# New matmul costs in the list scheduler of a two-block transformer kernel

## The chip, the cores and the metric

The kernel runs on one NeuronCore of a Trainium2 chip. The metric is the device time of one execution in microseconds; the kernel before was timed three times. Everything else that is said of time here comes from one profiled execution of the same kernel.

## What is computed

Two transformer blocks, one behind the other, on 512 tokens of width 1024, in float32, with a modulation vector that scales and shifts every norm:

```python
def reference(x, c, ...):
    x = first_block(x, c, ...)           # 2 layers: gated FFN, hybrid mixer, gated FFN
    return second_block(x, c_2, ctx_2, ...)  # 2 layers with 256 context tokens beside

# first block, a layer: each sublayer reads a modulated RMS norm
h = rmsnorm(x, g) * (1.0 + scale) + shift        # shift, scale, gate: columns of silu(c) @ w_mod + b_mod
f = (jax.nn.silu(h @ w_g) * (h @ w_u)) @ w_down  # FFN, 2816 hidden features
# mixer: sliding window attention with sinks, a gated linear recurrence, a short convolution

# second block, a layer: mixer (latent attention, then neighbourhood attention), layer norm,
# gated FFN with a convolution of three taps over the positions, layer norm
h_lat = layer_norm(DEEPNORM_ALPHA * h_lat + g1 * y, ln1_g[i], ln1_b[i])
```

The context tokens go through the first layer of the second block too; the second layer only reads them as keys and values.

## The kernel before

Features lie along the 128 partitions and tokens along the free axis, so the stream of 512 tokens is eight tiles of 128 by 512. Weights come from HBM as float32 blocks of 128 by 512 (256 KB). ScalarE rounds each block to a high part (`wh`, CAST) and VectorE subtracts that to a low part (`wl`), and every product is three TensorE matmuls in the rounded type fp32r: high by high, high by low, low by high (`mm3`, `lin`). A moving operand is 512 or 256 columns wide. 256 columns are half the tokens, which is how a norm over one half runs beside the products of the other (`parts`, `ffn_end`), or all tokens of the context. Transposes through the identity (`ident`) move 128 columns of plain float32. Column sums (`colsum`, tile `acc`) multiply 128 by 128 float32 with a column of ones and have one column.

The attention scores of two heads are grouped by `mm2x`: two matmuls over 128 rows, then two over 64 rows each, for the first block's window attention and the second block's neighbourhood attention.

A norm is a chain over all engines: squares on ScalarE, sums on VectorE or GpSimd (`acc`), the column sum on TensorE, about ten short VectorE operations for the reciprocal root (`rsqrt`, tile `c`), a transpose of that column on TensorE that spreads it over the partitions (`bcast`, `ident,c`), and the scaled and shifted halves on VectorE and ScalarE (`tm`, `hh`, `hl`).

The modulation vectors are products of a vector with large matrices, and they don't run on TensorE. Two 256 KB blocks per step (`mr`) are multiplied with the vector on VectorE, with a running sum, and one of each three products on GpSimd with the sum on ScalarE. Where the context needs its own modulation as well, each block is multiplied twice (`mj`, `b_cc`).

**The order of the work is made by the source.** `Recorder.call` takes every operation down in program order and gives it a cost in ns (`Recorder.cost`, line 178). `Recorder.schedule` (line 285) then simulates the five engines with these costs and a table of latencies between them: each engine, when free, takes the earliest operation of the program whose operands are ready and whose tiles have room. The order in which the simulation starts operations is the order in which `emit` issues them, and on the chip each engine runs its own list in that order, waiting where an operand is late. So a cost changes no instruction, only places in five lists.

The cost of TensorE is also a yardstick for the program order itself. `Recorder.call` sums it in `self.pe`. `Core.run` (line 855) reads the sum after each step of the main stream. It writes one step of the modulations into the program for each `EVERY` = 6150 ns of the main stream's TensorE cost, from 20000 ns on, and steps of the context's stream until these have cost 0.22 of the main stream's (0.2987 during the latent attention and after it); there VectorE's cost counts half. The context's stream starts when the modulation it needs has been written down. A step of the modulations that is needed earlier is written down on demand (`mod`).

Of the kernel before, what the change touches and what calls it, by code (L numbers as in the profile page):

```python
# [13 lines left out]
F32R = mybir.dt.float32r  # L14
# [5 lines left out]
P = 128  # L20
# [49 lines left out]


def parts(T):
    """The tokens in halves: a norm over one runs beside the products of the other."""
    return [slice(i, i + C) for i in range(0, T, C)]


# [9 lines left out]


class View:
    """A part of a tile that gets its memory once the order of the program is known."""

    __slots__ = ("t", "box", "ops", "flat", "raw", "size")

# [57 lines left out]


class Recorder:
    """Takes the program down op by op, then issues it in the order of a list schedule: each engine
    runs the earliest op of the program whose operands are there and whose tiles have room."""

    ENGINES = ("tensor", "vector", "scalar", "gpsimd", "sync")
    LAT = {"tensor": {"tensor": 0},
# [20 lines left out]
    def cost(self, eng, method, a, k):  # L178
        out = a[0]
        n = out.width() if isinstance(out, View) else a[1].width()  # L180
        if eng == "tensor":
            if method == "transpose":
                return 0.84 * n + 2
            x = a[2]
            return max(0.4167 * n, 107) + (3 if n > 256 else 4.5) if x.t.dt == F32R else 220
        if eng == "sync":
            rows = (out.box[1] - out.box[0]) if isinstance(out, View) else P
            return max(450, rows * n * 4 / 360)
        ins = [x for x in a[1:] if isinstance(x, View)]
        psum = any(x.t.psum for x in ins + [out])  # L190
        if method == "reduce_max":
            n = a[1].width()
        if eng == "scalar":
            extra = sum(93 for v in (k.get("bias"), k.get("scale"), k.get("accum_out")) if isinstance(v, View))
            return 95 + 0.75 * n + extra + (0 if psum else 0.08 * n)
        if eng == "vector":
            if method == "reciprocal":
                return 65 + 6.3 * n
            at = 65 + 60 * sum(isinstance(x, View) and x.width() == 1 for x in a[2:])
            if method in ("tensor_scalar", "memset") and not psum:  # L200
                return at + 0.53 * n
            return at + 1.05 * n
        if method == "tensor_scalar":
            return 160 + 0.836 * n + 95 * any(isinstance(x, View) for x in a[2:])
        return 150 + 2.1 * n
# [224 lines left out]


class Lag:
    """Puts the parts of a chain that wait for other engines behind the start of the next ones."""

    def __init__(self, n):
        self.n, self.q = n, []
# [17 lines left out]
class Core:  # L454
# [169 lines left out]
                    self.mcol[(kind + sfx, l, ch)] = cols  # L624

    def first_mods(self):
        """The first shift and scale, finished block by block of features."""
        nc = self.nc
        Sh, G = self.mods[:, 0:8], self.mods[:, 8:16]
        for m in range(8):  # L630
            nc.later = FIRST[0] + FIRST[1] * m
            dots = []
            for ch in range(2):
                d = [self.col(1), self.col(1)]
                for h in range(2):
                    raw = self.t(s="mr")
                    nc.sync.dma_start(raw, self.io["wmod"][0, ch * 8 + m][:, h * 512:(h + 1) * 512])
                    if (2 * ch + h) % 4 in FIRST_POOL:
                        nc.gpsimd.tensor_tensor(raw, raw, self.cb["c", h], op=ALU.mult)
                        nc.scalar.activation(raw, raw, AF.Identity, accum_out=d[h])  # L640
                        continue
                    nc.vector.scalar_tensor_tensor(raw, raw, 1.0, self.cb["c", h], op0=ALU.mult, op1=ALU.mult, accum_out=d[h])
                dots.append(d)
            for ch, out in enumerate((Sh, G)):
                nc.vector.scalar_tensor_tensor(out[:, m:m + 1], dots[ch][0], dots[ch][1], self.bmod[:, ch * 8 + m:ch * 8 + m + 1], op0=ALU.add, op1=ALU.add)
            nc.vector.scalar_tensor_tensor(G[:, m:m + 1], G[:, m:m + 1], 1.0, self.gn[:, m:m + 1], op0=ALU.add, op1=ALU.mult)
        nc.later = 0
        self.mcol["w", 0, 0] = Sh
        self.mcol["w", 0, 1] = G
# [85 lines left out]
        return copy[:, :T]  # L735

    def times(self, p, c):
        """Weights of a softmax times their sum's reciprocal."""
        self.nc.gpsimd.tensor_scalar(p, p, c, 1.0, op0=ALU.mult, op1=ALU.mult)

    def rms(self, x, T, width, eps=1e-6):
# [65 lines left out]
        yield from self.ffn_end(x, dn, prev, hid, gate, T, after)  # L807

    def ffn_end(self, x, dn, prev, hid, gate, T, after):
        """The products with the last two groups of hidden features, for half the tokens and then the others."""  # L810
        gate = self.mod(*gate)
        last = len(FF_CHUNKS) - 1
        a, b = {}, {}
        for sl in parts(T):
            for m in range(KD):
                if m not in a:
                    a[m] = self.wblk(dn, 8 * (last - 1) + m, kind="wend")
                if m // 2 not in b:
                    b[m // 2] = self.wblk(dn, 8 * last + m // 2, kind="wend")
                pd = self.ps()[:, :T]  # L820
                self.lin(pd, a[m] + b[m // 2][m % 2 * 2:m % 2 * 2 + 2], prev + hid, parts=(sl,))
                self.accum(x, m, pd, gate, sl)
                if m % 2:
                    yield
            if after is not None:
                yield from after(sl)
# [26 lines left out]
        return o  # L853

    def run(self, main, side):
        """Takes main down; between its steps, a step of the modulations for every `every` ns of tensor
        work and steps of side up to `share` of main's tensor work."""
        rec = self.nc
        mods, own = BEGIN, 0.0
        due = 0.0  # L860
        mark = rec.pe
        for _ in main:
            own += rec.pe - mark
            due += self.share * (rec.pe - mark)
            while mods + self.every <= own:
                mods += self.every
                next(self.modgen, None)
            while side is not None and due > 0:
                mark = rec.pe + HEAVY * rec.ve
                got = next(side, "end")  # L870
                due -= rec.pe + HEAVY * rec.ve - mark
                if got == "end":
                    side = None
                elif got == "wait":
                    due = 0.0
            mark = rec.pe

    def rms_part(self, l, sub):
        """The modulated norm before a sublayer of the first block, for some of the tokens at a time."""
        out = [self.pair(S, "h") for _ in range(KD)]  # L880

        def part(sl):
# [7 lines left out]
        return out, part  # L890

    def final_part(self):
        """The first block's last norm, then the second block's first modulation."""
        nc = self.nc
        out = [self.pair(S, "a") for _ in range(KD)]
        g = self.gn[:, 48:56]
# [189 lines left out]
                yield from after(sl)  # L1086

    def stack(self, hi, lo):
        """For two heads' halves of 64 rows: each head's high and low parts over one another."""
        nc = self.nc  # L1090
        n = hi.width()
        other = self.t(F32R, s="st")[:, :n]
# [3 lines left out]
        return hi, other  # L1096

    def twice(self, hi):
        """For two heads' halves of 64 rows: each head's rows two times over."""
        nc = self.nc  # L1100
        n = hi.width()
        other = self.t(F32R, s="tw")[:, :n]
# [3 lines left out]
        return hi, other  # L1106

    def mm2x(self, outs, qs, ks, lows):
        """Products of two heads: q's both parts with k's high part in one pass, its high part with
        k's low part in the other."""  # L1110
        te = self.nc.tensor
        rows = (slice(0, 64), slice(64, 128))
        self.nc.group()
# [69 lines left out]
        return output  # L1183

    def centre(self, x, T):
        """Shifts each token by about the mean of its features: a layer norm, which follows, is the
        same for any shift, and its variance loses no digits to a large mean."""
        nc = self.nc
        acc = self.total(x, T, dt=F32R)
        bc = self.ps()[:, :T]  # L1190
# [2 lines left out]
            nc.vector.tensor_tensor(x[k], x[k], bc, op=ALU.subtract)  # L1193

    def ln_part(self, xs, T, l, which, kind, mod, perm=False):
        """A layer norm, and the modulation after it, for some of the tokens at a time."""
        nc = self.nc
        n = C // P
        c0 = (l * 2 + which) * 16
# [61 lines left out]
        return View(b[0][0].t, (0, P, 0, 512)), View(b[0][1].t, (0, P, 0, 512)), b[0][2]  # L1261

    def values(self, cn, wv, ts):
        """Values of 8 heads for 128 tokens: for each head its high and low parts side by side, the
        other way round for odd heads, so that the high parts' rows are the head's own."""
        nc = self.nc
        pv = self.ps()
        for k in range(2):
# [267 lines left out]
            nc.sync.dma_start(View(self.rpbt.t, (0, 16 * P, 24 * cq, 24 * cq + 24), raw=out), View(ed.t, ed.box, raw=inp))  # L1536

    def na_values(self, g, a, ac):
        """Values of two pairs of heads, tokens along the partitions: the four blocks of the latent
        tokens, the three that lie half a block further, and the context's two."""  # L1540
        nc = self.nc
        ws = [self.wblk("nqkv", 12 * g + i) for i in range(4)]
        wide = [tuple(View(w[j][part].t, (0, P, j * P, j * P + 256), (("__getitem__", ((slice(0, P), slice(j * P, j * P + 256)),), {}),))
# [282 lines left out]
```

## Time and profile before

| quantity | value |
|---|---|
| time of three runs, median (lowest to highest) | 3641.77 us (3635.7 to 3643.74) |
| span of the profiled execution, first to last instruction | 3637.0 us |
| TensorE matmuls, busy | 3507.4 us, 96% of the span |
| VectorE busy | 2715.5 us, 75% |
| ScalarE busy | 1822.0 us, 50% |
| GpSimd busy | 794.7 us, 22% |
| DMA, mean | 129 GB/s |

The profile gives the span of its execution; no time of that execution as a whole stands beside it, and the median of the three runs is 4.8 us above the span. A busy matmul overlaps its neighbours: a matmul of 512 columns has a duration of 0.39 us in the records, while the next one starts 0.23 us after it. So the distance between starts is what a matmul costs, and idle time is what is left uncovered.

### The profile page before, as it was taken

How to read it: one execution, taken by the hardware profiler on the slowest of the kernel's cores; microseconds unless marked ns; L12 is line 12 of the kernel's file. 1: busy time of each engine (PE TensorE's matmuls, PEld its weight loads, DVE VectorE, ACT ScalarE, POOL GpSimd, SP SyncE). 2: the span in 40 equal slices, each digit the busy share in tenths (PEclk: the TensorE clock that was granted, in tenths of full speed). 3: DMA queues.
4: the chain of work that ended last, by engine and by line, in shares of the span. 5: the costliest groups of instructions: out<-in, count | busy, mean ns of one | idle time of the engine just before them, and what ended most of it. 6: DMA issues, size and time to landing. Idle time of an engine off the chain costs nothing.

```text
span 3637.0 us, 56958 instructions
## 1 busy us (share of the span) xinstructions
PE 3507.4 (96%) x19814; PEld 3057.1 (84%) x19814; DVE 2715.5 (75%) x5566; ACT 1822.0 (50%) x3939; POOL 794.7 (22%) x848
## 2 busy tenths in 40 slices
PE   6999999999999999999999999999999899989998
PEld 5888979878898879889888988888888888878887
DVE  8966799976597776986444589998667767786566
ACT  5434466455455644754333479785344444454332
POOL 3301142421022330230000034342000523240002
PEclk9999999999999999999999999999999999989999
DMA  9954254655356543553335322124333133233320
GB/s 316 312 157 148 82 184 148 218 182 162 103 191 197 187 132 119 193 160 116 105 108 143 107 59 58 48 68 133 110 96 105 53 100 85 76 94 103 98 87 24
DMA packets 272127, 469.86 MB, mean 129 GB/s; under 512 B 39136, under 2 KB 53472, under 8 KB 271840
## 3 DMA queue, kind: packets, MB, share of 16 engines
q1 hardware_dynamic: 271840, 466.23, 41.9%
q8 instruction: 156, 2.56, 0.3%
q14 instruction: 131, 1.07, 0.1%
HBM read 448.81 MB, written 5.50 MB: 125 GB/s over the span
## 4 chain that ended last, share of the span: by engine, by line
PE 79%; DVE 13%; issue 2%; ACT 2%; DMA 2%; POOL 1%; SPq 0%; POOLq 0%; DVEq 0%; ACTq 0%
PE ps L429 79%; DVE wl L429 2%; DVE c L429 2%; DVE mr L429 1%; DVE acc L429 1%; DVE x L429 1%; DVE mj L429 1%; DVE ptl L429 1%; DMA mr<-in_wmod 1%; POOL P L429 0%; DMA wr<-in_gu 0%; DVE pl L429 0%; DVE al L429 0%; POOL pc L429 0%; DVE yl L429 0%
## 5 line engine op out<-in xcount | busy, mean ns | idle before, releaser
L429 DVE TENSOR_TENSOR wl<-wr,wh 128x512 fp32r<-128x512 f32 (+1 forms) x1182 | 834.4, 729 | 163.0 <-ACT wh L429 134.1
L429 ACT CAST wh<-wr 128x512 fp32r<-128x512 f32 (+1 forms) x1182 | 676.6, 614 | 96.0 <-PE ps L429 61.2
L429 PE MATMUL ps<-hh,wh 128*128 128x512 f32 (+1 forms) x1864 | 692.9, 372 | 3.3 <-ACT wh L429 2.7
L429 PE MATMUL ps<-hl,wh 128*128 128x512 f32 (+1 forms) x1864 | 689.7, 370 | 6.3 <-DVE hl L429 6.2
L429 PE MATMUL ps<-hh,wl 128*128 128x512 f32 (+1 forms) x1864 | 688.0, 369 | 0.1
L429 PE MATMUL ps<-fh,wh 128*128 128x512 f32 (+1 forms) x1344 | 463.5, 345 | 0.0
L429 PE MATMUL ps<-fl,wh 128*128 128x512 f32 (+1 forms) x1344 | 462.0, 344 | 0.2 <-DVE fl L429 0.2
L429 PE MATMUL ps<-fh,wl 128*128 128x512 f32 (+1 forms) x1344 | 461.8, 344 | 0.0
L429 PEld LDWEIGHTS ps<-hl,wh 128*128 128x128 f32 x1864 | 355.4, 191 | 65.0 <-DVE hl L429 9.3
L429 PEld LDWEIGHTS ps<-hh,wh 128*128 128x128 f32 x1864 | 355.5, 191 | 60.8 <-ACT wh L429 3.1
L429 PEld LDWEIGHTS ps<-hh,wl 128*128 128x128 f32 x1864 | 355.1, 190 | 59.7 <-DVE wl L429 1.3
L429 DVE SCALAR_TENSOR_TENSOR x<-ps,mods,x 128x512 f32<-128x512 f32 (+1 forms) x400 | 254.9, 641 | 187.8 <-PE ps L429 186.1
L429 PE MATMUL ps<-ah,wh 128*128 128x512 f32 (+1 forms) x1000 | 366.9, 367 | 0.0
L429 PE MATMUL ps<-al,wh 128*128 128x512 f32 (+1 forms) x1000 | 365.3, 365 | 0.1
L429 PE MATMUL ps<-ah,wl 128*128 128x512 f32 (+1 forms) x1000 | 364.9, 365 | 0.0
L429 POOL TENSOR_TENSOR mr<-mr,b_c 128x512 f32<-128x512 f32 x123 | 179.0, 1457 | 515.1 <-DMA mr<-in_wmod 247.6
L429 DVE SCALAR_TENSOR_TENSOR cv<-ps,ffc,cv 128x511 f32<-128x511 f32 (+1 forms) x264 | 173.3, 659 | 143.7 <-ACT cv L429 140.1
L429 PEld LDWEIGHTS ps<-fl,wh 128*128 128x128 f32 x1344 | 254.7, 190 | 30.0 <-DVE fl L429 0.4
L429 PEld LDWEIGHTS ps<-fh,wl 128*128 128x128 f32 x1344 | 254.6, 189 | 30.1
L429 PEld LDWEIGHTS ps<-fh,wh 128*128 128x128 f32 x1344 | 254.7, 189 | 29.5
L429 ACT ACTIVATE cv<-ps,ffc 128x512 f32<-128x512 f32 (+1 forms) x132 | 93.4, 708 | 314.7 <-PE ps L429 314.0
L429 ACT CAST fh<-s 128x512 fp32r<-128x512 f32 x132 | 81.8, 621 | 299.1 <-DVE s L429 297.0
(332 smaller groups left out, 7115.6 us busy)
## 6 DMA issues: line engine op xcount, KB each, us to landing
wr<-in_gu SPq DMA_DIRECT2D x352, 256.0 KB, 2.9
mr<-in_wmod SPq DMA_DIRECT2D x288, 256.0 KB, 4.2
wr<-in_fin SPq DMA_DIRECT2D x264, 256.0 KB, 2.7
mr<-in_wada SPq DMA_DIRECT2D x192, 256.0 KB, 3.6
wr<-in_dn SPq DMA_DIRECT2D x176, 256.0 KB, 3.1
wr<-in_fout SPq DMA_DIRECT2D x132, 256.0 KB, 2.7
wr<-in_win SPq DMA_DIRECT2D x64, 256.0 KB, 3.3
wr<-in_nqkv SPq DMA_DIRECT2D x48, 256.0 KB, 2.9
```

Of the source, the lines that this page charges most:

```text
L429: getattr(eng, method)(*a, **k)
```

## The change

The diff replaces the cost of a TensorE matmul in `Recorder.cost`. The rest of the diff takes docstrings out and leaves the code as it is.

```diff
             if method == "transpose":
                 return 0.84 * n + 2
             x = a[2]
-            return max(0.4167 * n, 107) + (3 if n > 256 else 4.5) if x.t.dt == F32R else 220
+            if x.t.dt != F32R:
+                return 112
+            rows = a[1].box[1] - a[1].box[0]
+            return max(0.4167 * n, 107) + 13.4 if rows == P else 255
```

In ns, with `n` columns:

| form | cost before | cost after |
|---|---|---|
| fp32r, 512 columns, 128 rows | 216.4 | 226.7 |
| fp32r, 256 columns, 128 rows | 111.5 | 120.4 |
| fp32r, 64 rows, up to 256 columns | 111.5 | 255 |
| float32 column sum, one column | 220 | 112 |
| transpose of 128 columns | 109.5 | 109.5 |

`EVERY`, the shares and every other cost and latency stay as they are. No instruction is added or taken away.

## Rows read from the trace of the kernel before

**Rows 1.** The page's first line.
```profile
span 3637.0 us, 56958 instructions
```

**Rows 2.** Busy time in stretches: us, then PE, PEld, DVE, ACT, POOL, PEclk, DMA.
```profile
400.00:735.00 335.00, 309.67 (x1825) 271.76 (x1823) 323.72 (x749) 191.97 (x467) 122.80 (x97) 0.97 0.54 169
735.00:1200.00 465.00, 463.86 (x2487) 402.41 (x2488) 331.81 (x701) 245.29 (x527) 91.81 (x96) 1.00 0.54 168
1200.00:1320.00 120.00, 110.83 (x544) 93.27 (x543) 105.54 (x212) 69.87 (x152) 58.04 (x49) 0.96 0.48 150
1455.00:1620.00 165.00, 160.52 (x976) 139.63 (x976) 154.49 (x356) 118.54 (x278) 54.14 (x54) 1.00 0.59 186
2100.00:2500.00 400.00, 385.57 (x2643) 352.07 (x2643) 370.34 (x869) 313.25 (x751) 157.09 (x210) 0.99 0.22 64
2845.00:3260.00 415.00, 391.32 (x2553) 346.28 (x2551) 310.09 (x633) 191.88 (x435) 151.82 (x187) 0.96 0.30 83
```

**Rows 3.** Waits of TensorE, whole span: us in total, times, longest.
```profile
PE ps L429 <- DVE c L429: 35.8, 16, 9.9
PE ps L429 <- DVE acc L429: 28.5, 10, 11.1
PE ps L429 <- POOL P L429: 9.3, 10, 2.5
PE ps L429 <- DVE ptl L429: 8.1, 13, 1.9
```

**Rows 4.** Waits of TensorE, first 100 us and last 37 us.
```profile
PE ps L429 <- DVE acc L429: 11.1, 1, 11.1
...
PE ps L429 <- DVE c L429: 7.0, 2, 5.3
```

**Rows 5.** Timeline of TensorE, one norm: start, us, instruction, idle before it.
```profile
2664.18 0.48 PE L429 MATMUL ps<-ah,wh 128*128 128x512 f32 x1
...
2671.34 0.39 PE L429 MATMUL ps<-al,wh 128*128 128x512 f32 x1
2671.56 0.39 PE L429 MATMUL ps<-ah,wl 128*128 128x512 f32 x1
2673.32 0.43 PE L429 MATMUL ps<-ident,c 128*128 128x128 f32 x2 [1.36 <-DVE c L429]
```

**Rows 6.** Timeline of TensorE: 256 columns, then a score group of two heads.
```profile
2939.84 0.28 PE L429 MATMUL ps<-wh,ah 128*128 128x256 f32 x1
2939.96 0.28 PE L429 MATMUL ps<-wl,ah 128*128 128x256 f32 x1
...
2943.24 0.39 PE L429 MATMUL ps<-kh,qh 128*128 128x256 f32 x1
...
2943.98 0.39 PE L429 MATMUL ps<-kc,qh 128*128 128x256 f32 x1
```

**Rows 7.** Timeline of TensorE, four other norms: the matmul that came late.
```profile
415.67 0.69 PE L429 MATMUL ps<-ident,c 128*128 128x128 f32 x2 [4.00 <-DVE c L429]
...
735.20 0.69 PE L429 MATMUL ps<-ident,c 128*128 128x128 f32 x2 [9.92 <-DVE c L429]
...
1295.02 1.01 PE L429 MATMUL ps<-ones,acc 128*128 128x1 f32 x4 [4.43 <-DVE acc L429]
...
1306.63 0.43 PE L429 MATMUL ps<-ident,c 128*128 128x128 f32 x2 [2.28 <-DVE c L429]
```

**Rows 8.** DVE time of modulations by stretch, tile mr, then tile mj.
```profile
400.00:735.00 335.00, 99.92 (x246) 0.97 0.54 169
1200.00:1320.00 120.00, 32.24 (x76) 0.96 0.48 150
1455.00:1620.00 165.00, 23.85 (x68) 1.00 0.59 186
...
400.00:735.00 335.00, 43.54 (x110) 0.97 0.54 169
1200.00:1320.00 120.00, 16.48 (x38) 0.96 0.48 150
```

## The prediction

> **What bounds the kernel now.** I read the table of stretches first, because one share for the whole span hides everything here. Over the 3637.0 us [rows 1] TensorE is the bound nearly throughout: between 735 and 1200 us it is busy for 463.9 of 465 us with VectorE at 71% [rows 2]. There no order of the work can gain or lose anything. The time that an order can touch lies in a few stretches where TensorE falls idle: 400 to 735 us (25.3 us idle, VectorE 97% busy), 1200 to 1320 us (9.2 us idle, VectorE 88%), 1455 to 1620 us (4.5 us, VectorE 94%), the latent attention from 2100 to 2500 us (14.4 us, VectorE 93%) and the neighbourhood attention from 2845 to 3260 us (23.7 us, VectorE 75%) [rows 2]. Next the list of TensorE's waits. It names one kind of cause: TensorE reaches a norm's column sum or its transpose, or a softmax's transpose, before VectorE or GpSimd has delivered. The norm's waits are 35.8 us over 16 for `c` and 28.5 us over 10 for `acc`; those of the softmax that are shown are 9.3 us over 10 for `P` and 8.1 us over 13 for `ptl` [rows 3]. Since each engine runs a fixed list, TensorE stands at such an instruction even when products that could run lie behind it. Of the norm waits, 11.1 us at the start and 7.0 us at the end [rows 4] have no products to fill them, and no cost moves those.
>
> **What the change does to the plan.** No instruction is added or removed; the direct cost is nothing. Five lists are put in another order, because the simulated TensorE gets slower. By how much, and is that true? In the timeline, matmuls of 512 columns start 0.22 to 0.23 us apart [rows 5], and those of 256 columns 0.12 us apart [rows 6]. A score group of two heads (two matmuls over 128 rows, two over 64) takes 0.74 us from 2943.24 to 2943.98 [rows 6]. The costs before make these 0.216, 0.1115 and 0.446 us; the new ones 0.227, 0.120 and 0.751. So the new costs are right for this trace, and the old ones too low by 5%, 7% and 40%. The Trainium skill speaks against the change here: "TensorE: Matmul & The Clock Gate", section "Wait — 56ns, not 53.3ns?", gives warm matmuls of 512 columns a distance of 215.7 ns, which is the old cost; by it the new cost would be 5% too dear, and the case for a gain (the second rival) would have no ground; of the sum below only the small last term would fall away. The rows here show 0.22 to 0.23 us [rows 5], and the measurement decides.
>
> A truer cost of one engine does not by itself make a better order, and this is my main step. **Step one, the cover of the norms.** The plan puts as many products between a norm's column sum and its transpose as fit into the chain's planned length. At 2664 us that cover runs from the matmul at 2664.18 to the one at 2671.56, some 33 matmuls, and the transpose still comes 1.36 us late [rows 5]. In the plan those 33 cost 33 x 0.2164 = 7.14 us; on the chip they take 33 x 0.227 = 7.5 us. The old cost thus carried a hidden reserve of 0.35 us per chain, and even with it the transpose was late. With the new cost the plan fits only 7.14 / 0.2267 = 31.5 matmuls into the same chain; the reserve is gone and TensorE waits 0.35 us longer. I found the same kind of late matmul, with 4.00, 9.92, 4.43 and 2.28 us, at four other places [rows 7]. The middle of the kernel has 35.8 and 28.5 us less 11.1 and 7.0, over some 23 waits [rows 3, 4]. At 0.35 us each that is **+8 us**. Bounds: 0, if the plan itself had nothing left to put in front, and +12 where the cover is of 256 columns and shrinks by 8% (0.5 us each).
>
> **Step two, the softmax chains** lose their reserve in the same way: 23 waits for `P` and `ptl` [rows 3] and as many small ones of other tiles by my estimate from the rest of the list, each with a shorter cover, say 0.2 us: 9 us. But most lie where VectorE is the fuller engine [rows 2], and there a longer wait of TensorE is partly paid back, since VectorE doesn't stop. I take **+4**, bounds 0 to +9.
>
> **Step three, the modulations come earlier.** Their steps are written into the program every 6150 ns of planned TensorE work, and this work grows by 4.8% (512 columns) to 8% (256), some 5.5% for the mix. So at any place of the main stream 5.5% more steps have been written, and the context's stream, which waits for one of them, begins some 20 to 25 us earlier too. (Within the context's stream the share stays: its TensorE cost rises as the main stream's does.) From 400 to 735 us VectorE spends 99.9 + 43.5 = 143.4 us on modulations [rows 8]; 5.5% are 7.9 us. VectorE's idle time there is 335 - 323.7 = 11.3 us [rows 2], much of it in waits too short to use, and the 9.92 us at 735 us [rows 7] says that VectorE is behind its plan at the end of this stretch. I take **+6**, bounds 0 to +10. The same shift helps later. The steps done from 1200 to 1320 us (32.2 + 16.5 = 48.7 us of VectorE, most of them doubled) [rows 8] move about 60 to 70 us forward, into a stretch with 29% of VectorE free [rows 2], and away from the norm whose two matmuls are 4.43 and 2.28 us late [rows 7]: **-5**, bounds -9 to 0, the 9.2 us that TensorE is idle there. From 1455 to 1620 us, 23.9 us of modulations [rows 8] fall by about half: **-2**, bounds -4.5 to 0 by the idle time of TensorE [rows 2]. The queue of SyncE, which issues the loads in the planned order, moves with this: the modulations' loads stand some 5% earlier among the weights; DMA is at 0.48 to 0.59 in these stretches [rows 2], so that costs nothing.
>
> **Step four, fewer wrong turns of the other engines.** In a true plan VectorE and ScalarE reach a product's result less often before it is there. In the stretches that VectorE fills this would count, but VectorE's idle time there is only 11.3 us (400 to 735 us) and 29.7 us (2100 to 2500 us) [rows 2], and one or two of them is what 5% can give back: **-1**, bounds -10 to 0. The score groups, with 40% the form most corrected, lie in the stretch with the most idle time of TensorE, 23.7 us [rows 2], but VectorE has slack there, and I count nothing for them.
>
> **The sum** against the profiled execution: 8 + 4 + 6 - 5 - 2 - 1 = +10 us, so a span of 3647 us; with the 4.8 us that the median lies above that span, **3652 us**. All lower bounds together are -23.5 us and all upper ones +31.
>
> **The rivals.** *Nothing that counts*: the shifts cancel, since most of the span has a TensorE without gaps; 3642 us, within 7. For it: the parts of the sum have both signs. Against it: step one hits nearly every norm on the same side. *Faster*: the plan's TensorE is now true, so a late matmul becomes rarer, and the modulations leave the norm at 1290 to 1306 us and the second mixer. It would take the lower bounds of the later steps (-9 - 4.5) and half of step four's (-5), against +5 left of steps one and two: -13.5, or 3628 us. For it: the late matmuls at 735 and 1295 us stand where modulations crowd VectorE, and a shift of 5% can unlock one of them. Against it: what is late on TensorE is late because VectorE and GpSimd are slower than planned, and slowing the planned TensorE widens that gap. It decides by whether covers shrink at the norms. *Much slower*: the stretch from 400 to 735 us has no reserve on VectorE, and the added 7.9 us of modulations and the earlier context stream delay its norms one after the other, so that the 9.92 us wait doubles: +10 there above step three's 6, or 3662 us. It decides from the point where VectorE is over 99% busy there. *That the change does nothing* is excluded: the costs enter the order and the yardstick.
>
> **How the numbers follow.** Forecast (3652) 0.34, much slower (3662 and above) 0.11, nothing 0.28, faster 0.27. A measurement tells about 0.2% (7 us) from no change. Slower by over 0.2%: 0.45; within: 0.28; faster: 0.27. The range leaves out the ends where all bounds add up, and takes in the faster rival's time and a little of the much slower one's far side: 3625 to 3674 us.
>
> **What would show it.** In the profile after, TensorE's waits for `c` and `acc` in the middle should sum to more than the 46 us of before, with about as many waits; fewer matmuls should lie between the column sums and their transposes; of the 23.9 us of modulations from 1455 to 1620 us [rows 8] about half should be gone; VectorE from 400 to 735 us should be at least as full; and the wait of 4.43 us near 1295 us should shrink. The prediction is wrong if the covers keep their number of matmuls, or if the norms' waits fall in total while the modulations move as said.

## The result: slower by 1.4%

The changed kernel takes 3688.31 us (3684.8 to 3689.96), the kernel before 3640.47 us in the runs beside it: a ratio of 1.0138, with an interval of 1.0126 to 1.0150. The forecast had the direction, but its 3652 us is far off, and 3688 us lies beyond its range. The profiled execution took 3684.8 us, its span 3682.7 us, 45.7 us above that of before [rows 1].

First the page of the kernel after (its span and TensorE's line, busy time and share), and then the mean granted clock of TensorE, before and after.

```profile
span 3682.7 us, 56929 instructions
PE 3523.0 (96%) x19814; PEld 3070.1 (83%) x19814; DVE 2714.8 (74%) x5566; ACT 1810.4 (49%) x3934; POOL 782.8 (21%) x848
```
```profile
core 0: 3637.0 us, clock 0.988
```
```profile
core 0: 3682.7 us, clock 0.984
```

The work is the same: 19814 matmuls, 5566 VectorE instructions. TensorE was busy for 3507.4 us before and is for 3523.0 us now, 15.6 us more for the same matmuls; it was idle for 129.6 us and is for 159.7 us, 30.1 us more. These two make the 45.7 us. The clock accounts for most of the first. The granted clock has two levels here, full and half, so a mean of 0.988 is half speed for 2 x 0.012 x 3637 = 87 us, and a mean of 0.984 for 2 x 0.016 x 3682.7 = 118 us. Work loses half of the time that it spends at half speed, and TensorE stood idle in some of that time. By the clock's stretches in the two traces it worked at half speed for 61 us before and for 87 us after, so 13 of the 15.6 us are the clock's.

The stretches of [rows 2] in the kernel after (us, PE, PEld, DVE, ACT, POOL, clock, DMA). The later ones no longer hold quite the same work.

```profile
400.00:735.00 335.00, 300.25 (x1775) 264.57 (x1775) 324.94 (x756) 189.95 (x474) 122.02 (x100) 0.95 0.53 168
735.00:1200.00 465.00, 456.43 (x2451) 394.99 (x2450) 328.81 (x692) 243.11 (x526) 101.52 (x103) 1.00 0.53 165
1200.00:1320.00 120.00, 109.00 (x522) 90.96 (x522) 106.23 (x215) 61.59 (x136) 45.98 (x42) 0.94 0.55 170
1455.00:1620.00 165.00, 157.73 (x1041) 142.11 (x1041) 141.26 (x323) 101.23 (x231) 39.81 (x39) 1.00 0.47 147
2100.00:2500.00 400.00, 381.02 (x2596) 346.62 (x2595) 352.75 (x845) 309.45 (x746) 139.96 (x201) 0.99 0.21 61
2845.00:3260.00 415.00, 395.69 (x2515) 349.28 (x2513) 298.80 (x596) 192.91 (x426) 135.77 (x168) 0.97 0.30 83
```

TensorE's waits after (us in total, times, longest), to hold against [rows 3], and then two rows of before that [rows 3] doesn't have:

```profile
PE ps L432 <- DVE acc L432: 38.0, 8, 12.3
PE ps L432 <- DVE c L432: 24.4, 15, 5.3
PE ps L432 <- DVE ptl L432: 14.4, 19, 2.6
PE ps L432 <- DVE pl L432: 10.6, 8, 4.4
...
PE ps L432 <- POOL P L432: 6.3, 5, 2.3
...
PE ps L432 <- ACT pth L432: 5.2, 4, 2.8
```
```profile
PE ps L429 <- DVE pl L429: 2.4, 3, 1.1
...
PE ps L429 <- ACT pth L429: 0.8, 2, 0.5
```

The norms' waits for VectorE, `acc` and `c`, sum to 62.4 us after and 64.3 us before: in total they have not grown. The total hides a trade: the 9.92 us at 735 us [rows 7] are gone (no wait for `c` is longer than 5.3 us now), and a wait of 12.28 us for `acc` is new. The waits inside the attentions grew: `ptl` from 8.1 to 14.4 us, `pl` from 2.4 to 10.6 us and `pth` from 0.8 to 5.2 us. Two of the largest new waits sit in the first block's first mixer and at the norm behind it. This is the timeline of TensorE there, after (start, us, instruction, idle before it):

```profile
511.19 0.28 PE L432 MATMUL ps<-ph,vh 128*128 128x256 f32 x1
515.87 0.54 PE L432 MATMUL ps<-pl,vh 128*128 128x256 f32 x1 [4.40 <-DVE pl L432]
...
516.43 0.41 PE L432 MATMUL ps<-ph,vh 128*128 128x256 f32 x1
516.64 0.41 PE L432 MATMUL ps<-pl,vh 128*128 128x256 f32 x1
...
624.79 1.01 PE L432 MATMUL ps<-ones,acc 128*128 128x1 f32 x4 [12.28 <-DVE acc L432]
```

Behind the wait of 4.40 us the matmuls of 256 columns start 0.21 us apart, where 0.12 us is normal [rows 6]: that is the half clock (0.53 is the mean granted clock from 515.87 to 517.00 us). Now ScalarE's last rounding of `ph` ahead of the wait's end, and what VectorE did while TensorE stood for `pl`:

```profile
510.00 0.59 ACT L432 CAST ph<-ps 128x512 fp32r<-128x512 f32 x1 [0.16 <-PE ps L432]
```
```profile
511.77 0.68 DVE L432 TENSOR_TENSOR wl<-wr,wh 128x512 fp32r<-128x512 f32 x1
...
513.58 0.68 DVE L432 SCALAR_TENSOR_TENSOR mj<-mr,b_c 128x512 f32<-128x512 f32 x1
...
514.19 0.69 DVE L432 SCALAR_TENSOR_TENSOR mj<-mr,b_c 128x512 f32<-128x512 f32 x1
...
514.80 0.69 DVE L432 TENSOR_TENSOR ql<-ps,qh 128x512 fp32r<-128x512 f32 x1
515.40 1.01 DVE L432 TENSOR_TENSOR pl<-ps,ph 128x256 fp32r<-128x256 f32 x2
```

The `ph` that `pl` is made from was there at 510.6 us, and VectorE never stood still in the wait. It worked on a weight block that is needed later, on the recurrence (one of the rows left out) and on modulations of the second block (`mj`), and only then on the `pl` that TensorE stood for. The wait of 12.28 us at the norm shows the same. These are VectorE's time and instructions on modulations in that wait (us, VectorE, clock, DMA), and then, before the change, in the same length of time ahead of the same column sum, for which TensorE waited 1.0 us there:

```profile
612.51:624.79 12.28, 6.16 (x12) 0.60 0.28 85
```
```profile
567.09:579.37 12.28, 0.10 (x2) 1.00 0.33 97
```

Half of that wait is modulations between the sums of the norm; the other half is the sums themselves and the updates of `x` that feed them.

### The profile page after: what moved, and what is told of

It reads as the page before. It is cut to its first block, busy times and chain, and to the rows that moved or that the text cites. A ratio compares the mean times of both kernels' runs of the same rounds, so it can differ in the third digit from the quotient of the medians.

```text
span 3682.7 us, 56929 instructions
## 1 busy us (share of the span) xinstructions
PE 3523.0 (96%) x19814; PEld 3070.1 (83%) x19814; DVE 2714.8 (74%) x5566; ACT 1810.4 (49%) x3934; POOL 782.8 (21%) x848
## 4 chain that ended last, share of the span: by engine, by line
PE 53%; DVE 8%; ACT 3%; issue 1%; DMA 0%; POOL 0%; SPq 0%; POOLq 0%; DVEq 0%; ACTq 0%
PE ps L432 53%; DVE c L432 2%; DVE wl L432 1%; DVE x L432 1%; DVE ptl L432 1%; DVE acc L432 1%; DVE pl L432 0%; ACT pth L432 0%; ACT pl L432 0%; DVE al L432 0%; DVE mr L432 0%; DVE cv L432 0%; ACT L432 0%; ACT Qh L432 0%; ACT pc L432 0%
## 5 line engine op out<-in xcount | busy, mean ns | idle before, releaser
L432 DVE TENSOR_TENSOR wl<-wr,wh 128x512 fp32r<-128x512 f32 (+1 forms) x1182 | 844.4, 733 | 172.5 <-ACT wh L432 143.5
L432 PEld LDWEIGHTS ps<-fh,wl 128*128 128x128 f32 x1344 | 255.0, 190 | 30.3
```

Source lines behind the costliest of these rows:

```text
L432: getattr(eng, method)(*a, **k)
```

## The experiments

Every kernel here computes the whole thing; only the simulated costs, and with them the five lists, differ. "Plan" are the costs of the simulated engines, "pace" is the yardstick `self.pe` of `run`. All ratios are to the kernel before beside them, with a 95% interval.

| run | plan | pace | median us | ratio (interval) |
|---|---|---|---|---|
| after | new | new | 3688.3 | 1.0138 (1.0126 to 1.0150) |
| e1 | new | old | 3681.9 | 1.0124 (1.0109 to 1.0139) |
| e2 | old | new | 3644.9 | 1.0026 (1.0015 to 1.0037) |
| e3 | new, all other costs x 1.055 | old | 3663.5 | 1.0075 (1.0060 to 1.0090) |
| e4 | matmuls x 1.015 | old | 3669.3 | 1.0091 (1.0074 to 1.0108) |
| f1 | matmuls x 0.985 | old | 3651.9 | 1.0041 (1.0028 to 1.0054) |
| f2, f3 | jitter of 1.5%, two draws | old | 3639.9, 3637.6 | 1.0012 (1.0003 to 1.0021), 1.0000 (0.9991 to 1.0010) |
| f4 | small forms new | old | 3660.2 | 1.0064 (1.0047 to 1.0081) |
| g1 | wide forms new | old | 3667.5 | 1.0088 (1.0073 to 1.0103) |
| g2 | wide forms new, all others x 1.055 | old | 3657.3 | 1.0060 (1.0045 to 1.0075) |
| g3 | 64 rows new | old | 3646.7 | 1.0026 (1.0015 to 1.0038) |
| g4 | column sums new | old | 3653.8 | 1.0055 (1.0038 to 1.0071) |
| h1, h2 | jitter of 10%, two draws | old | 3657.8, 3656.5 | 1.0056 (1.0041 to 1.0071), 1.0048 (1.0033 to 1.0063) |
| h3 | matmuls x 1.003 | old | 3639.9 | 1.0012 (1.0002 to 1.0021) |
| h4 | new, 0.4 us of reserve | old | 3675.0 | 1.0104 (1.0089 to 1.0119) |
| i1 | matmuls x 0.945 | old | 3636.8 | 1.0001 (0.9992 to 1.0010) |
| i2 | new, with h1's jitter | old | 3696.2 | 1.0162 (1.0145 to 1.0179) |

**Plan or pace?** The edit of e1 keeps the old cost in the yardstick and takes the new one for the simulated operation (`self.new` picks the formula in `cost`); e2 swaps the two values. e3 is e1 with the costs of all other engines, the latencies and the waiting times of the simulation times 1.055, and e4 multiplies the old matmul costs by 1.015 in the plan alone.

```diff
+        self.new = False
         cost = self.cost(eng, method, a, k)
         if eng == "tensor":
             self.pe += cost
+            self.new = True
+            cost = self.cost(eng, method, a, k)
```

> The simulated engines use the new matmul costs; the yardstick that paces modulations and context stream keeps the old ones, so the program order is that of the kernel before. Before 3640 us, after 3688 us. Covers (the slower planned TensorE puts fewer products in front of late norms and softmaxes): 3675 to 3690 us, nearly all of the loss. Pace (modulations and context come 5.5% earlier into stretches that VectorE fills): 3640 to 3655 us. Scatter (the order before was a lucky one and any other order costs some tens of us): 3660 to 3700 us.

> The reverse: the simulated engines keep the old matmul costs, the yardstick counts with the new ones, so modulations and context stream come earlier in the program by some 5.5%. Covers: 3640 to 3650 us. Pace: 3675 to 3690 us. Scatter: 3660 to 3700 us, as for any other order.

> New matmul costs in the simulated engines, old yardstick, and every other cost and latency of the simulation times 1.055, so that TensorE stands to the other engines about as before. Covers (the ratio is what counts): back to 3635 to 3655 us while the run with the new matmul costs alone stays slow. Pace: 3640 to 3655 us like that run. Scatter: 3660 to 3700 us, no nearer to the kernel before than the others.

> Old costs and old yardstick, but the simulated matmuls cost 1.5% more, about a quarter of the change. Covers: a quarter of the loss at most, 3640 to 3655 us. Pace: 3640 us, nothing of it changed. Scatter: 3655 to 3700 us, as much as the whole change.

The plan alone loses 1.24%, the pace alone 0.26%, and both together 1.38%. But e4, with about a quarter of the change, already costs 0.91%, and e3, which restores most of the proportion between the engines, still 0.75%. That is not a loss in proportion to the price; it spoke for a third theory, that any other order costs some tens of us.

**Which way, and how much of it is jitter?** f1 makes the simulated matmuls cheaper (`cost *= 0.985`). f2 and f3 draw a factor for each operation by its place in the program, here with a span of 1.5%. f4 gives only the small forms their new costs.

```diff
         if eng == "tensor":
             self.pe += cost
+            cost *= 1 + 0.015 * (2 * (len(self.ops) * 7919 * 1 % 101 / 100) - 1)
```

> Old costs and yardstick, the simulated matmuls 1.5% cheaper, so that the covers gain reserve. The run with 1.5% dearer ones was 0.9% slower than before. Covers: no slower than before, 3625 to 3645 us. Scatter: as slow as the 1.5% dearer plan, 3655 to 3690 us.

> Old costs and yardstick, each simulated matmul's cost off by a number between -1.5% and +1.5% that is drawn by its place in the program, so that the mean stays. Covers: 3635 to 3650 us, since no chain loses its reserve. Scatter: 3655 to 3690 us, as for the plan that is dearer on all.

> The same with other draws. Covers: 3635 to 3650 us. Scatter: again 3655 to 3690 us, but some 10 us off the first draw.

> Only the small forms get their new costs in the simulated engines (255 ns over 64 rows, 112 ns for the column sums); the wide matmuls and the yardstick keep the old ones. The small forms lie in the two mixers of the first block, at the norms and in the neighbourhood attention. Covers: 3635 to 3655 us, since the products that cover the chains keep their cost. Scatter: 3650 to 3690 us, and also in the latent attention, where no small form stands.

Small jitter costs next to nothing (0.12 and 0.00%), which spoke against the third theory, and matmuls 1.5% cheaper cost 0.41%, which spoke against the first, the covers. The small forms alone, which aren't the products that cover a chain, cost 0.64%.

**Form by form.** g1 and g2 take the wide forms alone, without and with the other costs scaled; g3 and g4 take the two small forms one at a time.

> Only the matmuls of 512 and 256 columns get their new costs in the simulated engines (+4.8% and +8%); the small forms and the yardstick stay. With all forms it was 1.24% slower than before, with the small forms alone 0.64%. Ratio (what counts is how TensorE stands to the other engines in the plan): 0.5 to 0.9% slower, 3654 to 3669 us. Small forms alone to blame: within 0.2% of before. Any shift of the mean costs the same whatever its size (1.5% dearer cost 0.9%, 1.5% cheaper 0.4%): 0.4 to 0.9% too, so this run does not tell that from ratio; the next one does.

> The same, and every other cost and latency of the simulation times 1.055, small forms included, so that the plan is nearly the old one on a slower clock (512 columns 0.7% under it, 256 columns 2.4% over it, transposes unscaled). Ratio: within 0.3% of before, 3630 to 3647 us, while the run with dearer wide matmuls alone is slower by over 0.4%. Any shift costs: 0.4 to 0.9% slower, 3650 to 3669 us.

> Only the matmuls over 64 rows get the new cost (255 for 111.5 ns) in the simulated engines. They stand in the first block's two mixers and in the neighbourhood attention. If the 0.64% of the small forms is theirs: 3652 to 3664 us, lost at the first block's mixers. If it is the column sums': 3632 to 3645 us.

> Only the column sums get the new cost (112 for 220 ns) in the simulated engines, which makes each norm's chain 0.4 to 0.9 us shorter in the plan. If the 0.64% of the small forms is theirs, through fewer products in front of each late transpose: 3650 to 3664 us, spread over the norms. If it is the score groups': 3632 to 3645 us.

Each form alone costs something (0.88, 0.26 and 0.55%), and they don't add up to the 1.24% of all. g2 speaks against the ratio as the whole cause: in proportion its plan is nearly the old one, and 0.60% are lost all the same.

**Any order, or a dearer TensorE?** h1 and h2 are f2 and f3 with a span of 10%; h3 multiplies by 1.003; h4 is e1 with 0.4 us more in the latencies from VectorE, ScalarE and GpSimd to TensorE:

```diff
-           "vector": {"vector": 135, "scalar": 140, "gpsimd": 165, "tensor": 215},
-           "scalar": {"vector": 140, "scalar": 143, "gpsimd": 170, "tensor": 200},
-           "gpsimd": {"vector": 80, "scalar": 80, "gpsimd": 102, "tensor": 170},
+           "vector": {"vector": 135, "scalar": 140, "gpsimd": 165, "tensor": 615},
+           "scalar": {"vector": 140, "scalar": 143, "gpsimd": 170, "tensor": 600},
+           "gpsimd": {"vector": 80, "scalar": 80, "gpsimd": 102, "tensor": 570},
```

> Old costs and yardstick, each simulated matmul off by a drawn number between -10% and +10%, the mean unchanged. Shift of the mean (covers, ratio): within 0.3% of before, 3628 to 3648 us, as the jitter of 1.5%. Any other order: 0.4 to 1.0% slower, 3650 to 3675 us.

> The same with other draws. Shift of the mean: within 0.3% of before. Any other order: 0.4 to 1.0% slower, 3650 to 3675 us, and not the same as the first draw.

> Old costs and yardstick, the simulated matmuls 0.3% dearer. Shift of the mean in proportion (1.5% lost 0.91%): 0.18%, 3643 us. Any other order: it goes by how much of TensorE's list moves, so from nothing to 0.6%, 3636 to 3658 us, out of proportion to the shift.

> New costs in the simulated engines, old yardstick (1.24% slower than before without more), and every result of VectorE, ScalarE and GpSimd reaches the simulated TensorE 0.4 us later, so that the plan puts some 0.4 us more of products in front of each of TensorE's waits, about what the covers were to have lost at a norm. Covers: at least a third of the loss comes back, 3665 us or less, and TensorE's waits for VectorE fall. Any other order: 3655 to 3690 us, with no preference.

With the mean untouched, both draws of 10% lose about 0.5%. So an order that differs enough can cost that much by itself. h3 lies at 0.12%, which fits both forecasts. The reserve in front of TensorE's operands brings back 0.2 of 1.24%, where the cover theory wanted at least a third, and the two intervals overlap: covers are not the main thing.

The last two runs part the two effects. i1 makes the matmuls 5.5% cheaper (`cost *= 0.945`), as far from the old price as the new one is. i2 puts h1's draw on the new costs.

> Old costs and yardstick, the simulated matmuls 5.5% cheaper, so that covers hold 5.5% more products. Covers on top of any other order: less than the 0.5% of the jitter, 3635 to 3654 us. Any other order alone: 0.4 to 1.3% slower, 3650 to 3683 us, since the order moves as far as with the new costs.

> New costs in the simulated engines with the jitter of 10% of the first draw, old yardstick. Covers on top of any other order: 1.0 to 1.5% slower, 3672 to 3690 us, as without jitter, with the loss in the first mixer again. Any other order alone: 0.3 to 0.9%, 3647 to 3669 us, as the jitter of the old costs.

i1 loses nothing. i2 loses 1.62%, more than either forecast, where h1, the same draw on the old costs, loses 0.56%. So on top of the 0.5% of another order, dearer matmuls in the plan cost 0.7% (e1) to 1.1% (i2), and the cheaper ones of i1 seem to give the 0.5% back; that is one run, and f1, cheaper by 1.5%, did lose 0.41%. It fits that e3 and g2, where the ratio of the engines is nearly the old one, come down to 0.75 and 0.60%, near the 0.5% of jitter. e4 with its 0.91% doesn't fit well: by its price it should have lost little more than jitter.

**Where each effect sits.** For this table I took from each trace the distance from every matmul's start to the next one's, less the normal distance of its form (0.227 us for 512 columns, 0.120 for 256, 0.120 also over 64 rows, 0.112 for a column sum, 0.109 for a transpose). The rest, in us, is waiting, half clock and what score groups take beyond that. It is summed between the same amounts of normal matmul work, so that the same stage is compared in each run.

| stage (normal work, us) | before | after | e2 | e1 | i2 | h1 | h2 | i1 |
|---|---|---|---|---|---|---|---|---|
| start (0 to 300) | 28.8 | 29.7 | 27.6 | 28.5 | 29.0 | 28.1 | 28.3 | 28.1 |
| first mixer, its norms (300 to 700) | 40.0 | 54.4 | 44.3 | 53.4 | 58.4 | 45.3 | 42.0 | 43.6 |
| two FFNs, their norms (700 to 1300) | 17.3 | 29.4 | 17.9 | 19.7 | 22.4 | 16.3 | 17.1 | 11.3 |
| second mixer (1300 to 1600) | 12.9 | 14.9 | 8.5 | 25.9 | 19.3 | 15.3 | 21.0 | 8.2 |
| latent attention (2000 to 2500) | 28.5 | 43.0 | 38.9 | 40.1 | 44.5 | 40.6 | 43.1 | 41.1 |
| neighbourhood attention (2700 to 3200) | 62.2 | 64.9 | 60.0 | 67.0 | 67.4 | 58.5 | 57.4 | 55.2 |
| whole span | 201.6 | 246.5 | 207.6 | 248.1 | 253.1 | 216.0 | 220.5 | 198.3 |

Two patterns stand out. In the latent attention all seven other orders of the table lose 10 to 16 us against the one before, dearer, cheaper or jittered: that is the larger part of what another order costs. (The jitter of 1.5%, which is small beside the prices, has 28.2 and 31.8 there; of the other runs h3 and g3 have 28, and f1, f4, g2, g4 and e3 have 34 to 36.) In the first mixer, the second and the neighbourhood attention the runs with a dearer TensorE (e1, i2) lose 13 to 18, 6 to 13 and 5 us, while the cheaper one (i1) loses 4 and gains 5 and 7. The second mixer is the least clear of the three, since one jittered run (h2) loses 8 us there too. The changed kernel itself loses 14.4, 2.0 and 2.7 us in these three. It also loses 12.1 us in the two FFNs, where e1 and e2, with one half of the change each, lose 2.4 and 0.6: from 735 to 1260 us its waits for `ptl` and `pth` sum to 9.5 us, where before has 2.5 us and e1 2.5 us. So that part needs both halves of the change; what makes it was not tested.

How much of each loss is waiting and how much is TensorE's own busy time? Here are TensorE's lines of the pages of e1, e4 and h1:

```profile
PE 3530.8 (96%) x19814; PEld 3075.1 (83%) x19814; DVE 2715.9 (74%) x5566; ACT 1819.3 (49%) x3939; POOL 788.1 (21%) x848
```
```profile
PE 3532.4 (96%) x19814; PEld 3078.1 (84%) x19814; DVE 2719.2 (74%) x5566; ACT 1820.7 (50%) x3938; POOL 789.8 (21%) x848
```
```profile
PE 3509.3 (96%) x19814; PEld 3058.5 (84%) x19814; DVE 2729.2 (75%) x5566; ACT 1822.1 (50%) x3939; POOL 786.0 (22%) x848
```

Their spans are 3683.3, 3673.7 and 3651.3 us. Against before, e1 has 23.4 us more of busy time for the same matmuls and 22.9 us more of idle time, e4 25.0 and 11.7 us, h1 1.9 and 12.4 us. So h1 loses by waiting, while half of e1's loss and two thirds of e4's are busy time, at mean clocks of 0.984 and 0.981 for the 0.988 of before.

**What a dearer TensorE does in the first mixer.** Here is that mixer in seven runs, from the column sum of the norm ahead of it to the first one behind it, 918 to 928 matmuls in each: before, i1, h1, e4, e3, e1 and i2. Each fence has all engines first (us, PE, PEld, DVE, ACT, POOL, clock, DMA), then VectorE's time and instructions on the modulations: the row of the tile `mr`, which holds those that write `mj` too, since they read `mr`. A product is two instructions.

```profile
406.40:579.40 173.00, 160.07 (x922) 137.92 (x920) 162.48 (x384) 109.86 (x278) 66.46 (x61) 0.97 0.43 134
406.40:579.40 173.00, 35.71 (x92) 0.97 0.43 134
```
```profile
406.80:570.60 163.80, 157.31 (x918) 134.85 (x916) 153.99 (x361) 104.54 (x263) 61.09 (x59) 0.99 0.41 129
406.80:570.60 163.80, 33.92 (x88) 0.99 0.41 129
```
```profile
405.90:579.40 173.50, 159.55 (x924) 135.95 (x922) 163.26 (x382) 108.67 (x278) 68.21 (x61) 0.99 0.43 133
405.90:579.40 173.50, 40.64 (x92) 0.99 0.43 133
```
```profile
405.90:589.30 183.40, 165.67 (x928) 141.64 (x926) 167.01 (x393) 110.01 (x279) 67.73 (x62) 0.94 0.42 132
405.90:589.30 183.40, 39.56 (x98) 0.94 0.42 132
```
```profile
406.20:587.90 181.70, 164.28 (x924) 139.28 (x923) 166.64 (x399) 110.03 (x280) 72.64 (x63) 0.96 0.44 138
406.20:587.90 181.70, 40.43 (x104) 0.96 0.44 138
```
```profile
408.90:592.50 183.60, 162.29 (x926) 138.07 (x926) 178.78 (x415) 111.15 (x286) 78.17 (x67) 0.97 0.45 142
408.90:592.50 183.60, 50.40 (x122) 0.97 0.45 142
```
```profile
409.90:601.20 191.30, 169.32 (x923) 143.68 (x923) 180.53 (x413) 112.53 (x288) 78.34 (x67) 0.93 0.43 134
409.90:601.20 191.30, 50.45 (x120) 0.93 0.43 134
```

Before has 92 / 2 = 46 modulation products in this mixer, i1 44, h1 46, e4 49, e3 52, e1 61 and i2 60; the mixer takes 173.0, 163.8, 173.5, 183.4, 181.7, 183.6 and 191.3 us. The program order is the same in all seven. In e1 the plan's VectorE has more room beside the dearer matmuls, and the list puts 15 more products into it that nobody in this mixer needs. On the chip VectorE has little room: it was already busy for 162.5 of 173 us and is now for 178.8 of 183.6. The plan prices a product at 65 + 1.05 x 512 = 603 ns. Most follow one another at 0.61 us (513.58 to 514.19 above), but some take over 1 us each (5 of 45 before, 9 of 60 in e1), so that the mean busy time of one was 35.71 / 46 = 0.78 us before and 50.40 / 61 = 0.83 us in e1.

The count follows the price of the matmuls against that of the other engines. The jittered run with the old mean has the old count, and where the other costs rise too it falls back: e3 has 52 for e1's 61, and g2 has 47 for g1's 55. The time does not follow the count in step. e4 with 3 more products than before loses as much here (10.4 us) as e1 with 15 more (10.6 us), although its VectorE is busy for only 167.0 of 183.4 us; 5.6 of e4's 10.4 us are TensorE's busy time at a clock of 0.94. f4, with the old price on all wide matmuls, has 49 products and takes 183.1 us. e3 gives 9 of the 15 products back and only 1.9 us of the time. At the norm behind the mixer the filling does stand on the path with the plan alone: e1's wait for `acc` is 7.11 us there, and this is VectorE's time on modulations in it.

```profile
585.36:592.47 7.11, 3.80 (x6) 0.71 0.32 106
```

So the filling is shown, and about half of that wait is its work; that it is the main cost of dearer matmuls is not shown. No run held the products in their places while the matmuls got dearer.

The second mixer, in the same cut, before and in e1, has no such filling:

```profile
1460.10:1639.70 179.60, 176.38 (x1088) 154.73 (x1089) 161.08 (x374) 122.29 (x286) 51.58 (x52) 1.00 0.54 169
```
```profile
1475.90:1668.60 192.70, 185.50 (x1092) 162.68 (x1092) 161.41 (x372) 122.11 (x286) 49.67 (x52) 0.95 0.49 155
```

VectorE's work is the same (161 us), and of the 13.1 us 9.1 are busy time of TensorE for nearly as many matmuls: a clock of 0.95 for 1.00, beside idle time that is 4.0 us longer (7.2 for 3.2 us).

## Why the prediction failed

**The direction** was right, and in part for the reason given: VectorE's results come late on TensorE, and a slower planned TensorE made that worse. The size was not: +10 us were forecast, and the span grew by 45.7 us. Two things failed: step one, which was the largest term and came to nothing in the norms' waits, and the sum, which left out the half clock and what another order costs by itself.

**Step one (covers of the norms, +8).** The covers did shrink as said. At the norm of [rows 5], e1 has 30 matmuls in place of 33:

```profile
2704.75 0.48 PE L438 MATMUL ps<-ah,wh 128*128 128x512 f32 x1
...
2711.23 0.39 PE L438 MATMUL ps<-al,wh 128*128 128x512 f32 x1
2711.45 0.39 PE L438 MATMUL ps<-ah,wl 128*128 128x512 f32 x1
2713.08 0.32 PE L438 MATMUL ps<-ident,c 128*128 128x128 f32 x1 [1.24 <-DVE c L438]
```

From 2704.75 to 2711.45 is 6.70 us, 29 distances of 0.23. Yet the transpose is 1.24 us late and not the 1.7 us that the step gives, and over the kernel the norms' waits went from 64.3 to 62.4 us (65.6 us in e1), where I had +8. The step's error was to charge every shorter cover to the path. The chain's own length isn't fixed: it depends on what the plan puts between its VectorE operations. In the wait of 12.28 us these were 6.16 us of modulations, and at 735 us the wait of 9.92 us went away. h4 agrees from the other side: putting the reserve back returned 0.2 of 1.24%.

**Step two (softmax chains, +4)** was mis-sized. `ptl`, `pl`, `pth` and `P` together went from 20.6 to 36.5 us, which is 15.9 us where I had +4 and at most +9. In e1, where the plan alone is new, they have 30.3 us. I priced a cover that is 0.2 us shorter; in the one wait that is opened above, at 515.87 us, VectorE's list had other work in front of the result.

**Step three (pace, +6 - 5 - 2).** e2 measures it: +0.26%, 9 us. The table gives +4.3 us for the first mixer, where I had +6, and -4.4 us for the second, where I had -2. The -5 us at the norm near 1295 us didn't come (17.3 and 17.9 us over these FFNs), and the latent attention took +10.4 us, where I had nothing. One reading under this step was wrong: the rows of `mr` in [rows 8] hold those of `mj` already, so VectorE spent 99.9 us on modulations from 400 to 735 us and not 143.4, and 32.2 us from 1200 to 1320 us and not 48.7. With 5.5 us in place of 7.9 the +6 would have been a little smaller.

**Step four (fewer wrong turns, -1)** can't be told from the rest: no run measures it by itself, and TensorE's idle time grew by 30.1 us. It asked only whether the other engines would be misled less often. A slower planned TensorE also shows the planner room on VectorE, and the planner filled it in the first mixer (46 products became 61 in e1). No term of mine had that. How many of the 45.7 us it makes is not measured.

**What had no term at all.** The busy time that comes with the half clock: 15.6 of the 45.7 us, 23.4 us in e1. And another order as such: about 0.5%, 18 us, in h1 and h2, most of it in the latent attention. All upper bounds of the steps end at 3642 + 31 = 3673 us, so the range to 3674 us reached just that far and had no room for an order that is merely different, though TensorE's waits in the latent attention were short and could hardly shrink. Of the rivals, "much slower" was the nearest in its place (VectorE in the first mixer) but priced at less than half of what came. Of the signs I had named, some came: covers shorter, yes; VectorE from 400 to 735 us at least as full, yes (324.9 us for 323.7); modulations gone from the second mixer in part (17.4 us of `mr` after, between its norms, by the same cut as the 23.0 us of before); more waits of the norms, no, and their fall in total was one of the two signs of being wrong.

**On the price itself.** The distances are still those that the new costs say (2711.23 to 2711.45 above); this one price is truer and the kernel is slower. i1, with a price 10% under the measured distance, is as fast as the kernel before. A price in this planner acts as a weight between engines, whatever it measures.

**What stays open** is, first, why e4 and f4 lose as much in the first mixer as e1 with few products added. Second, what makes the order before so good in the latent attention: its excess of 28.5 us was met by none of the seven orders in the table, and no single wait makes the difference. No version here beats the kernel before.

## What to carry to other kernels

In a list scheduler, a price that is corrected for one engine alone also changes what the planner puts into the lists of the others: here it filled VectorE with work that was early and not needed yet, and half of the largest new wait was that work. Raising the other prices with it (e3) gave back 0.5 of the 1.24%; a cap on the early work was not tried. Before explaining a few per cent after such a change, measure what a meaningless change costs: jitter of 10% around the same mean cost 0.5% here, jitter of 1.5% next to nothing. And read which engine's list a price lengthens or fills, not only the engine that it prices.

## What the runs showed of the hardware

Idle time of TensorE can cost more than itself. From before to after 30.1 us of added idle time came with 15.6 us of added busy time for the same 19814 matmuls, as the mean granted clock fell from 0.988 to 0.984. In the second mixer of e1 the added busy time was larger than the added idle time: 9.1 us beside 4.0, at a clock of 0.95 for 1.00. There is no fixed ratio between the two: over the whole kernel e4 added 25.0 us of busy time to 11.7 us of idle time, and h1 1.9 us to 12.4.
